# Summing the squares of a norm on TensorE instead of VectorE, in a two-layer diffusion block on one core

## The chip, the core and the metric

The kernel runs on one NeuronCore of a Trainium2 chip. A core has five engines that work in parallel, each through its own queue in order: PE (TensorE, the matrix engine; the loads of its stationary operand are shown apart as PEld), DVE (VectorE), ACT (ScalarE), POOL (GpSimd) and SP (SyncE, which issues the transfers here). They wait for each other by semaphores. PE writes into PSUM, which has eight banks of 128 x 512 floats; the other data lie in SBUF, 128 partitions wide. The metric is the device time of one execution in microseconds (us), the median over several.

## The reference, cut to what matters

The program is one pass of a small diffusion backbone: 512 latent and 256 context tokens of width 1024, two layers. Layer 0 mixes tokens by gated linear attention, layer 1 by neighbourhood attention; each is followed by a gated MLP with a width-3 convolution. Ahead of each of the four sub-layers, and at the end, stands an RMS norm:

```
def rms_norm(x, g):
    xf = x.astype(jnp.float32)
    y = xf * lax.rsqrt(jnp.mean(xf * xf, axis=-1, keepdims=True) + EPS)
    return (y * g.astype(jnp.float32)).astype(x.dtype)

def modulate(x, g, shift, scale):
    return rms_norm(x, g) * (1 + scale) + shift
```

In layer 1 the context tokens are only read, so that from there on the norms cover the 512 latent tokens alone. All is computed in float32.

## The kernel before, in words

Activations lie transposed: features on the partitions, tokens along the free axis. The 1024 features are eight tiles of 128 rows, so a norm has to sum eight squares elementwise and then sum over the 128 partitions. Weight products are made in three passes of a split operand (high and low parts, `mm3`, lines 274 to 277): each product that the text names is three matmuls, L275, L276 and L277.

The class `Norm` does the norms, for a range of tokens of width w = 512 or 256. There are ten of them at five places: before the linear attention (latent 512, then context 256), before the first MLP (`finish_gla`), between the first MLP and the neighbourhood stage (`last_outs(0, ...)`), between the neighbourhood stage and the second MLP (two halves of 256 latent tokens), and the final norm (two halves of 256).

`add(k)` is called when tile k of x is final: ACT squares it (L320 straight into the sum `nacc` for the first tile, L323 into a scratch tile `sq` for the other seven), and DVE adds each of those seven into the sum (L324). At two of the places the sum is a part of a tile named `apad`, and the scratch tiles are T2h, T3h, T4l and the like. `stats()` sums over the partitions on PE: for each 128 tokens one matmul with the squares as stationary operand and two columns of ones as moving operand (L331; each such float32 matmul is two records in the trace). Then DVE scales (`ms`, L333), POOL takes the power -0.5 (`rs`, L335), PE spreads the result over the partitions by a product with the identity (L338), and at the start ACT copies it to SBUF (`rb`, L342). `apply(k)` multiplies and splits tile k into the `hh` and `hl` of the next products (DVE L358, ACT L359, DVE L360).

At the places within the program the tile of x is made by a product on PE, added to the residual by DVE (`add_gated`, L299), squared by ACT, and so on; the norm of one range is applied while the products of the next range run (`todo`). L147, L150, L155 and L128 belong to `ada_first`, which makes the first layer's shift and scale; L270 and L271 split weight tiles into their high (`wh`, ACT) and low (`wl`, DVE) parts; L234 and L145 are transfers of weights.

The order on each engine is not that of the source: the framework that builds the program schedules it by its own estimate of durations, and each engine then runs its list strictly in order. So an edit in the norm also moves instructions around it. Scratch tiles and PSUM banks rotate; the norm at the start has four scratch tiles.

## Time and profile before

| what | value |
|---|---|
| time, median of 3 runs | 1723.74 us |
| the three runs | 1716.87, 1723.74, 1723.84 us |
| profiled execution, its own time | 1716.47 us |
| span of its trace | 1714.7 us |
| PE busy | 96% of the span |
| DVE, ACT, POOL busy | 69%, 43%, 12% |

In the rows below, a timeline row reads: start in us, duration in us (of a merged row, from the first start to the last end), engine, line, operation, out<-in, shape, count, and in brackets how long the engine sat idle before it and which instruction ended that. A window row gives busy time and count for PE, PEld, DVE, ACT and POOL, then the granted TensorE clock, the share of busy transfer engines and GB/s. Matmuls are pipelined: a product on 256 columns is shown as 0.28 us long, but the next one starts 0.12 us later.

### The profile page before, as it was taken

Reading aid. Unit: us, or ns where it says so; the run is one execution under the profiler, and the core shown is the slowest. Engines: PE = TensorE matmul, PEld = TensorE weight load, DVE = VectorE, ACT = ScalarE, POOL = GpSimd, SP = SyncE. Lnnn points to the kernel's source line nnn. Section 1 sums busy time; section 2 is a strip of 40 time slices with the busy share of each in tenths; the row PEclk is TensorE's granted clock in tenths of the full one; section 3 lists DMA queues with packets and bytes.
Section 4 is the critical chain, followed back from the end, with each engine's and each line's share of the span. In section 5 each row is a group of like instructions: output and inputs, shape, how many; then the busy total and the mean of one; then the engine's idle time right before and its main releaser. Section 6 shows DMA issues by size and latency. Waiting matters only on the chain.

```text
span 1714.7 us, 27141 instructions
## 1 busy us (share of the span) xinstructions
PE 1648.3 (96%) x10867; PEld 1412.8 (82%) x10867; DVE 1187.9 (69%) x1973; ACT 740.0 (43%) x1331; POOL 206.6 (12%) x321
## 2 busy tenths in 40 slices
PE   5999999999999999999999989999999999999997
PEld 3768778777899999999999868887877888888887
DVE  4797877775997877978767774647476755555555
ACT  3665756563753342433434543433344522222332
POOL 1031212320000000000000042433332000000000
PEclk9999999999999999999999989999999999999999
DMA  7653523014333332524223051415141232322321
GB/s 259 193 173 101 172 73 107 20 50 136 99 120 113 114 109 74 172 64 145 89 72 110 26 192 48 147 47 160 43 135 38 85 96 91 99 87 86 110 86 50
DMA packets 54190, 179.70 MB, mean 105 GB/s; under 512 B 7024, under 2 KB 10864, under 8 KB 54064
## 3 DMA queue, kind: packets, MB, share of 16 engines
q1 hardware_dynamic: 54064, 177.97, 32.5%
q8 instruction: 85, 1.39, 0.3%
q14 instruction: 41, 0.34, 0.1%
HBM read 173.75 MB, written 2.10 MB: 103 GB/s over the span
## 4 chain that ended last, share of the span: by engine, by line
PE 72%; DVE 11%; ACT 5%; issue 4%; DMA 4%; POOL 3%; SPq 0%; POOLq 0%; DVEq 0%; ACTq 0%
PE mm L275 14%; PE mm L276 14%; PE mm L277 14%; PE aux L275 8%; PE aux L276 8%; PE aux L277 8%; DMA sa<-in 2%; PE mm L1236 1%; PE aux L1219 1%; POOL bias L1132 1%; PE aux L637 1%; DVE acc L200 1%; DVE t L558 1%; PE aux L1194 1%; DMA st<-in 1%
## 5 line engine op out<-in xcount | busy, mean ns | idle before, releaser
L275 PE MATMUL mm<-hh,wl 128*128 128x512 f32 (+3 forms) x864 | 307.2, 358 | 4.6 <-ACT hh L359 2.5
L276 PE MATMUL mm<-hl,wh 128*128 128x512 f32 (+3 forms) x864 | 302.2, 350 | 0.0
L277 PE MATMUL mm<-hh,wh 128*128 128x512 f32 (+3 forms) x864 | 301.9, 350 | 0.0
L275 PE MATMUL mm<-uh,wl 128*128 128x512 f32 (+1 forms) x544 | 189.0, 349 | 0.0
L276 PE MATMUL mm<-ul,wh 128*128 128x512 f32 (+1 forms) x544 | 188.8, 347 | 0.2 <-DVE ul L288 0.2
L277 PE MATMUL mm<-uh,wh 128*128 128x512 f32 (+1 forms) x544 | 188.9, 348 | 0.0
L275 PEld LDWEIGHTS mm<-hh,wl 128*128 128x128 f32 (+1 forms) x864 | 163.1, 189 | 28.9 <-issue 5.0
L270 ACT ACTIVATE wh<-st 128x1024 fp32r<-128x1024 f32 (+1 forms) x127 | 131.8, 1051 | 114.8 <-issue 69.4
L299 DVE SCALAR_TENSOR_TENSOR xl<-mm,mod,xl 128x512 f32<-128x512 f32 (+1 forms) x168 | 116.2, 698 | 93.8 <-PE mm L277 92.9
L276 PEld LDWEIGHTS mm<-hl,wh 128*128 128x128 f32 (+1 forms) x864 | 163.7, 189 | 18.0 <-issue 1.0
L277 PEld LDWEIGHTS mm<-hh,wh 128*128 128x128 f32 (+1 forms) x864 | 163.3, 189 | 18.1 <-issue 0.4
L275 PE MATMUL aux<-hh,wl 128*128 128x384 f32 (+2 forms) x496 | 173.7, 351 | 0.0
L276 PE MATMUL aux<-hl,wh 128*128 128x384 f32 (+2 forms) x496 | 173.6, 350 | 0.0
L277 PE MATMUL aux<-hh,wh 128*128 128x384 f32 (+2 forms) x496 | 173.4, 350 | 0.0
L271 DVE TENSOR_TENSOR wl<-st,wh 128x1024 fp32r<-128x1024 f32 (+1 forms) x126 | 153.8, 1227 | 22.7 <-ACT wh L270 22.3
L250 ACT ACTIVATE wh<-st 128x512 fp32r<-128x512 f32 (+1 forms) x126 | 94.1, 756 | 164.9 <-issue 56.9
L335 POOL TENSOR_TENSOR rs<-ms,mhalf 128x2 f32<-128x2 f32 (+1 forms) x10 | 10.9, 1094 | 930.8 <-DVE ms L333 930.8
L275 PEld LDWEIGHTS mm<-uh,wl 128*128 128x128 f32 x544 | 102.8, 189 | 15.7 <-ACT uh L287 2.0
L276 PEld LDWEIGHTS mm<-ul,wh 128*128 128x128 f32 x544 | 103.0, 189 | 14.7 <-DVE ul L288 0.4
L277 PEld LDWEIGHTS mm<-uh,wh 128*128 128x128 f32 x544 | 102.8, 189 | 13.2
L251 DVE TENSOR_TENSOR wl<-st,wh 128x512 fp32r<-128x512 f32 (+1 forms) x126 | 104.7, 848 | 13.0 <-ACT wh L250 12.7
L275 PEld LDWEIGHTS aux<-hh,wl 128*128 128x128 f32 x496 | 93.5, 189 | 8.6 <-issue 1.2
(330 smaller groups left out, 3251.3 us busy)
## 6 DMA issues: line engine op xcount, KB each, us to landing
st<-in SPq DMA_DIRECT2D x201, 512.0 KB, 3.7
sa<-in SPq DMA_DIRECT2D x98, 512.0 KB, 4.1
sx<-in SPq DMA_DIRECT2D x14, 512.0 KB, 6.3
xl<-in SPq DMA_DIRECT2D x8, 512.0 KB, 6.5
xc<-in SPq DMA_DIRECT2D x4, 512.0 KB, 8.4
out<-y SPq DMA_DIRECT2D x16, 128.0 KB, 1.7
raw<-in SPq DMA_DIRECT2D x16, 96.0 KB, 2.5
t<-q SPq DMA_DIRECT2D x16, 64.0 KB, 2.2
```

The source lines that it names most:

```text
L200: nc.vector.scalar_tensor_tensor(acc[0], st, cs[:, k, c:c + 1], acc[0], OP.mult, OP.add)
L250: nc.scalar.activation(hi, s_, AF.Copy)
L251: nc.vector.tensor_sub(lo, s_, hi.bitcast(F32))
L270: nc.scalar.activation(hi, st, AF.Copy)
L271: (eng or nc.vector).tensor_sub(lo, st, hi.bitcast(F32))
L275: mm(out, a[1], b[0], start=first, stop=False, **at)
L276: mm(out, a[0], b[1], start=False, stop=False, **at)
L277: mm(out, a[0], b[0], start=False, stop=last, **at)
L299: nc.vector.scalar_tensor_tensor(x_, ps, gate(l, n, d, rng), x_, OP.mult, OP.add)
L558: nc.vector.tensor_mul(ek, ek, st[h]["k"])
L637: mm(ps[:, 0:DV], a_, b_, start=i == 0, stop=i == len(terms) - 1)
L1132: nc.gpsimd.tensor_tensor(bt[ps_, o2:o2 + 192], rv[ps_], nmask[ps_, var, 64 * half:64 * half + 192], OP.add)
```

## The change

The sum of the squares may now be made in PSUM. A new method `total` issues the matmuls with ones; PE accumulates over several of them in one bank. In most norms six squares are still added on DVE and the eighth is handed to PE by itself, so that `stats` issues two groups of matmuls, one on the sum and one on the last square. At the place between the neighbourhood stage and the second MLP (`pe=True`) there is no DVE sum at all: each of the eight squares gets its own group as soon as it is there. The tile `nacc` is not allocated there.

```diff
         def add(self, k):
 
-            if self.first:
-                self.first = False
+            self.count += 1
+            if self.count == 1 and not self.pe:
                 if self.acc is None:
                     self.acc = self.pool.tile([128, self.w], F32, name="nacc", tag=f"nacc{self.w}", bufs=2)
                 nc.scalar.activation(self.acc, xk(k, self.rng), AF.Square)
                 return
             sq = self.tmp("sq")
             nc.scalar.activation(sq, xk(k, self.rng), AF.Square)
-            nc.vector.tensor_add(self.acc, self.acc, sq)
+            if self.pe:
+                self.total(sq)
+            elif self.count < KD:
+                nc.vector.tensor_add(self.acc, self.acc, sq)
+            else:
+                self.last = sq
+
+        def total(self, sq, last=False):
+
+            first = self.ps is None
+            if first:
+                self.ps = ps_aux()
+            for i in range(self.w // 128):
+                mm(self.ps[:, 2 * i:2 * i + 2], sq[:, i * 128:(i + 1) * 128], ones, start=first and i == 0,
+                   stop=last or self.count == KD and self.pe, skip_group_check=True)
 
         def stats(self):
 
             c = self.w // 128
-            ps = ps_aux()
-            for i in range(c):
-                mm(ps[:, 2 * i:2 * i + 2], self.acc[:, i * 128:(i + 1) * 128], ones, start=True, stop=True)
+            if not self.pe:
+                self.total(self.acc)
+                self.total(self.last, True)
+            ps = self.ps
...
         todo = []
-        nacc = pool.tile([128, D], F32, name="nacc", tag="acc", bufs=1)
         for a, b in ((0, 256), (256, 512)):
-            norm = Norm(pool, 1, 1, (N_CTX + a, N_CTX + b), acc=nacc[:, a:b])
+            norm = Norm(pool, 1, 1, (N_CTX + a, N_CTX + b), pe=True)
             for d in range(KD):
                 out_group(3, d, a, b)
```

In the changed file the lines of `Norm` lie lower: L331 becomes L339, L338 becomes L355, L323 becomes L325, L342 becomes L359 and L359 becomes L376.

How the order moves, first on PE at the start of the program, before (`nacc` is the sum, `rs` the reciprocal root, `sx` the weights of the first shift and scale):

```order
L331 MATMUL aux<-ones,nacc 128x2 x4
L338 MATMUL aux<-ident,rs_160 128x128 x4
L331 MATMUL aux<-ones,nacc 128x2 x2
L147 MATMUL mm<-sx,cs 32x256
L338 MATMUL aux<-ident,rs_197 128x128 x2
L147 MATMUL mm<-sx,cs 32x256 x15
```

and now:

```order
L339 MATMUL aux<-ones,nacc 128x2 x4
L339 MATMUL aux<-ones,sq 128x2 x4
L355 MATMUL aux<-ident,rs_163 128x128 x4
L339 MATMUL aux<-ones,nacc 128x2 x2
L339 MATMUL aux<-ones,sq 128x2 x2
L147 MATMUL mm<-sx,cs 32x256
L355 MATMUL aux<-ident,rs_201 128x128 x2
L147 MATMUL mm<-sx,cs 32x256 x15
```

Each group on the sum is followed by an equal group on the last square, and all else stands as it did.

On ACT at the same place, before (xc_81 and xc_82 are the context tiles, `rb` the copy of the spread root):

```order
L320 ACTIVATE nacc<-xc_81 128x256
L323 ACTIVATE sq<-xc_81 128x256 x3
L323 ACTIVATE sq<-xc_82 128x256 x4
L342 ACTIVATE rb<-aux 128x512
L270 ACTIVATE wh<-st 128x512
L342 ACTIVATE rb<-aux 128x256
```

and now:

```order
L322 ACTIVATE nacc<-xc_81 128x256
L325 ACTIVATE sq<-xc_81 128x256 x3
L325 ACTIVATE sq<-xc_82 128x256 x2
L359 ACTIVATE rb<-aux 128x512
L325 ACTIVATE sq<-xc_82 128x256 x2
L270 ACTIVATE wh<-st 128x512
L359 ACTIVATE rb<-aux 128x256
```

The last two squares of the context range now stand behind the copy of the latent range's root.

On ACT between the neighbourhood stage and the second MLP, in the second half of the tokens, now (`xl` are the latent tiles, two features' tiles in each; the squares of the second half begin in the first row; before, single squares and single `hh` rows took turns here):

```order
L325 ACTIVATE sq<-xl_4196 128x256 x2
L376 ACTIVATE hh<-hf,mod_120 128x256 x2
L325 ACTIVATE sq<-xl_4197 128x256 x2
L376 ACTIVATE hh<-hf,mod_120 128x256
L325 ACTIVATE sq<-xl_4198 128x256
L376 ACTIVATE hh<-hf,mod_120 128x256
L270 ACTIVATE wh<-st 128x1024
L325 ACTIVATE sq<-xl_4198 128x256
L270 ACTIVATE wh<-st 128x1024
L376 ACTIVATE hh<-hf,mod_120 128x256 x2
L325 ACTIVATE sq<-xl_4199 128x256 x2
L376 ACTIVATE hh<-hf,mod_120 128x256 x10
```

Two weight copies (`wh`) now stand between the fourth and the fifth `hh`, with one square between them.

## The prediction

> **What bounds the kernel now.** I read the engines' share of the span first, then the chain of work that ended last, then the instructions at each of the five places with a norm.

> ```profile
> span 1714.7 us, 27141 instructions
> PE 1648.3 (96%) x10867; PEld 1412.8 (82%) x10867; DVE 1187.9 (69%) x1973; ACT 740.0 (43%) x1331; POOL 206.6 (12%) x321
> PE 72%; DVE 11%; ACT 5%; issue 4%; DMA 4%; POOL 3%; SPq 0%; POOLq 0%; DVEq 0%; ACTq 0%
> ```

> PE is busy 96% of the span and carries 72% of the chain; DVE, which the change relieves, is busy 69% and carries 11%. So work that moves from DVE to PE costs time wherever PE does not wait, and can only pay where PE waits for DVE. Such places are the start, the stretch between the neighbourhood stage and the second MLP, and the last microseconds. At the start the chain of waits, read in order of time, passes through the norm itself:

> ```profile
> 12.58 0.70 DVE nacc L324
> ...
> 13.41 1.85 PE aux L331 x8
> ...
> 18.53 0.44 DVE nacc L324
> 19.01 1.03 PE aux L331 x4
> ...
> 21.45 1.22 PE aux L338 x4
> 22.67 3.60 PE mm L147 x30
> ...
> 28.50 0.76 DVE hf L358
> ```

> The reader is to see that no slack lies here: the last latent add, its matmuls with ones (eight records), the last context add and its four records, the spread root (L338), and only then the products for the first shift (L147), since PE takes them in order; the first `hf` of the program (28.50) hangs on these.

> **The start.** Timeline rows of the same stretch, and its window:

> ```profile
> 15.37 3.59 DVE L324 TENSOR_TENSOR nacc<-nacc,sq 128x256 f32<-128x256 f32 x7
> 15.53 1.12 POOL L335 TENSOR_TENSOR rs<-ms,mhalf 128x4 f32<-128x4 f32 x1 [14.44 <-DVE ms L333]
> 16.70 2.07 PE L338 MATMUL aux<-ident,rs 128*128 128x128 f32 x8 [1.46 <-POOL rs L335]
> 18.81 0.60 ACT L342 ACTIVATE rb<-aux 128x512 f32<-128x512 f32 x1 [1.52 <-PE aux L338]
> 13.00:21.00 8.00, 5.90 (x22) 4.67 (x22) 4.09 (x11) 2.83 (x7) 1.81 (x2) 1.00 1.02 408
> ```

> Latent range: one add of 0.70 goes, and a second group of eight records comes, as long as the first (1.85). So its end, 15.26, moves by -0.70 + 1.85 = +1.15. The scale and the power (1.12) and the eight records of L338 (2.07) follow it, and the copy `rb` ends at 18.81 + 0.60 + 1.15 = 20.56 instead of 19.41. Context range: its seven adds ended at 18.96 and did not care about `rb`, because ACT made all seven squares before that copy. In the new order the last two squares stand behind it on ACT. So square six ends at about 20.56 + 0.42 = 20.98, the sixth add (0.44) at 21.4, and two groups of four records (1.03 each) end at 23.5, where one ended at 20.04. That is **+3.4** on the path to L147 and so to everything behind it. If ACT had kept its order, the context adds would start 1.15 later, be one fewer, and the extra group would give 1.15 - 0.44 + 1.03 = +1.7.

> This rests on 0.23 per record (1.85 by 8). Later in the program a group of four takes 0.36, 0.09 per record (1327.09 to 1327.45 in the next fence). With 0.09 the latent end moves by -0.70 - 1.85 + 16 x 0.09 = -1.1, `rb` ends at 18.3, square six at 18.7, its add at 19.2, eight records at 19.9: -0.1. These are the ends, -0.1 and +3.4; I take +3.4, because the slow rows are at this very place. The clock column of the window speaks for the other end: it shows 1.00 granted. [...]

> **Between the neighbourhood stage and the second MLP.** Timeline rows of PE and ACT, and two windows:

> ```profile
> 1323.00 0.39 PE L275 MATMUL mm<-oh,wl 128*128 128x256 f32 x1 [0.31 <-DVE xl L299]
> ...
> 1327.09 0.50 PE L331 MATMUL aux<-ones,nacc 128*128 128x2 f32 x4
> 1327.45 0.37 PE L275 MATMUL mm<-oh,wl 128*128 128x256 f32 x1
> 1327.65 0.28 PE L276 MATMUL mm<-ol,wh 128*128 128x256 f32 x1
> 1327.77 0.28 PE L277 MATMUL mm<-oh,wh 128*128 128x256 f32 x1
> ...
> 1328.64 0.71 PE L338 MATMUL aux<-ident,rs 128*128 128x128 f32 x4 [0.35 <-POOL rs L335]
> ...
> 1332.90 0.39 PE L275 MATMUL mm<-oh,wl 128*128 128x256 f32 x1 [1.66 <-DVE xl L299]
> ...
> 1333.56 1.06 ACT L270 ACTIVATE wh<-st 128x1024 fp32r<-128x1024 f32 x1 [0.20 <-PE mm L277]
> ...
> 1334.51 0.35 PE L275 MATMUL mm<-hh,wl 128*128 128x256 f32 x1 [0.63 <-DVE xl L299]
> 1334.53 0.49 ACT L359 ACTIVATE hh<-hf,mod 128x256 fp32r<-128x256 f32 x1
> ...
> 1341.42 0.71 PE L338 MATMUL aux<-ident,rs 128*128 128x128 f32 x4 [1.25 <-POOL rs L335]
> ...
> 1327.00:1342.00 15.00, 11.10 (x87) 10.24 (x86) 12.85 (x33) 8.22 (x18) 2.32 (x2) 1.00 0.03 3
> 1342.00:1356.00 14.00, 14.00 (x119) 14.00 (x118) 10.89 (x22) 6.87 (x14) 0.19 (x4) 1.00 0.26 78
> ```

> The price of one group on 256 tokens: it starts at 1327.09, the next product at 1327.45, and the one behind that 0.20 later instead of the usual 0.12 (1327.65 to 1327.77). So a group takes 0.36 to 0.44 of PE, and I use 0.40. There were two groups, there are sixteen: 14 x 0.40 = 5.6. Each of the 14 adds that go takes 0.43 on DVE (row in the last fence), but that pays only where PE waited for DVE: 0.31, 1.66 and 0.63, together 2.6. The brackets count from the modelled end of the product before (0.28 after its start) although the next could have started after 0.12, so each wait is 0.16 longer in truth: 3.1. With DVE free of the adds and PE slower I expect all three to go. The two waits for the power (0.35 and 1.25) stay, as POOL is as fast as before; the second shrinks by 0.24, because six products stand between its groups and L338 now, four before.

> One wait is new. The weight copies of ACT wait for a slot that one of the last products of this stage frees (1333.56). Before, `hh` and squares stood between the two copies; now, between the fourth and the fifth `hh`, come a copy, one square, a copy: 1.06 + 0.42 + 1.06, then 0.49 for the `hh`, 3.0 in all after the slot comes free. Behind it on ACT are the sixth `hh` and the last two squares, and DVE's `hl` waits for each `hh`. PE needs that fifth `hh` after some 16 products and a group, 16 x 0.12 + 0.40 = 2.3. So PE waits 0.7 for `hh`, and about as long again as that `hh` (0.5) for the `hl` that follows; part of that is absorbed if PE is late by then. I take 1.0. Sum: 5.6 - 3.1 - 0.2 + 1.0 = **+3.3**. Ends: 14 x 0.36 = 5.0, less all waits for DVE and POOL (3.1 + 1.6) = +0.3; 14 x 0.44 = 6.2 with the new wait at 1.4 and no wait removed = +7.6. Nothing behind absorbs it: in the window from 1342 to 1356 PE is busy 14.00 of 14.00.

> **Ahead of the first MLP, and behind it.** Rows of PE at these norms:

> ```profile
> 425.59 0.95 PE L331 MATMUL aux<-ones,apad 128*128 128x2 f32 x8
> 426.39 0.36 PE L275 MATMUL mm<-hh,wl 128*128 128x256 f32 x1
> 426.60 0.28 PE L276 MATMUL mm<-hl,wh 128*128 128x256 f32 x1
> ...
> 452.93 0.58 PE L331 MATMUL aux<-ones,apad 128*128 128x2 f32 x4 [0.70 <-DVE apad L324]
> 454.78 0.71 PE L338 MATMUL aux<-ident,rs 128*128 128x128 f32 x4 [0.26 <-POOL rs L335]
> ...
> 964.06 1.46 PE L338 MATMUL aux<-ident,rs 128*128 128x128 f32 x8 [0.82 <-POOL rs L335]
> ...
> 983.34 0.71 PE L338 MATMUL aux<-ident,rs 128*128 128x128 f32 x4 [1.20 <-POOL rs L335]
> ...
> 964.00:966.00 2.00, 1.94 (x12) 1.94 (x13) 0.82 (x2) 0.00 (x0) 0.01 (x1) 0.69 0.00 0
> 966.00:968.00 2.00, 2.00 (x11) 2.00 (x11) 1.36 (x4) 1.72 (x3) 0.00 (x0) 0.50 0.00 0
> ```

> Ahead: the latent group (eight records) takes 425.59 to 426.60 less 0.12 = 0.89, and PE does not wait there for the sum, so +0.9. The context group waited 0.70 for its sum and 0.26 for the power, 1.3 with the correction of about 0.16 each. Now the group on the sum stands some 15 products earlier, five products lie between it and the square, and 15 more ahead of L338: both waits go, and 0.40 comes: -0.9. Together 0.0. Behind: latent +0.89, less 0.24 because six products instead of four cover the power (0.82 idle); context +0.40, less 0.7 because six products on 512 columns (twice 0.12 each) instead of three cover it (1.20 idle): **+0.4** together. Between -1 and +2.

> **The end.** The last rows of the chain:

> ```profile
> 1704.38 0.42 ACT L323 ACTIVATE sq<-xl 128x256 f32<-128x256 f32 x1 [1.00 <-DVE xl L299]
> 1704.83 0.43 DVE L324 TENSOR_TENSOR nacc<-nacc,sq 128x256 f32<-128x256 f32 x1
> 1705.31 0.61 PE L331 MATMUL aux<-ones,nacc 128*128 128x2 f32 x4 [1.54 <-DVE nacc L324]
> ```

> The last add leaves the path: the group on the square can start at 1704.85 instead of 1705.31, and that on the sum has run before. -0.45; the first half of the final norm gets a group among PE's products, +0.1. **-0.35**, between -0.6 and 0.

> **Sum.** 3.4 + 0.0 + 0.4 + 3.3 - 0.35 = +6.8. The profiled execution took 1716.47 (span 1714.7 and 1.8 around it), so it would take 1723.3. But the runs shown lie on two levels, 1716.9 and 1723.8, and the profile on the lower one. With the mean of these four, 1720.2, I predict **1727.0**, 0.4% more than before, inside the 0.5% (8.6 us) that a measurement of this kernel can tell from no change.

> **The rivals.**

> - *ACT's queue decides the stretch ahead of the second MLP* (slower). The copies and squares ahead of the fifth `hh` hold PE, and waits for DVE only change their name. Price +7.6 there, 3.4 + 0.4 + 7.6 - 0.35 = +11.1, 1731.3. For it: ACT is in order, and the slot comes free only with the last product. Against: ACT is busy only 8.22 of the 15.00 from 1327 to 1342. It decides from the point at which PE reaches the fifth `hh` sooner than 3.0 after the slot is free. 0.25.
> - *The start runs at full pace.* -0.1 there instead of +3.4: +3.3, 1723.5. For it the clock column, against it the rows. 0.12.
> - *DVE was the bound.* All waits in that stretch go, and the start is at its low end: -0.1 + 0.4 + 0.3 - 0.35 = +0.3, 1720.5. 0.08.
> - *A clock dip goes away.* The window 964 to 966 shows 0.69 granted, the next one 0.50, right behind a wait of 0.82. At half clock for some 4 us PE loses about 2.0. A shorter wait may spare it: +4.8, 1725.0. 0.10. [...]

> The forecast has 0.40; 0.05 is left for a reordering that I have not priced (the lists differ for some stretches into the first MLP too).

> **How the numbers follow.** The low end, 1718, holds the low-end case and the lower level of the runs; the high end, 1736, the ACT rival with the upper level of the runs (1723.8 + 11.1 = 1734.9). Slower by over 0.5%: most of the first rival and the forecast's upper tail, 0.30. Faster by over 0.5% needs a gain that no row offers, or a change of level: 0.06. The rest, 0.64, is within 0.5%.

> **What would show it.** Right: two equal groups of ones back to back at 12 to 16 us; the first `hf` at about 31.9 instead of 28.5; PE busier between 1317 and 1345 with no wait for `xl`, yet the second MLP starting some 7 us later than before; a new wait of a product for `hh` or `hl` there; the last scale (L333) 0.5 sooner after its last square. Wrong: a start under 1 us later than before, records of 0.09 at the start, or waits for `xl` that stay. The prediction falls if the whole is under 1718, that is if PE's added groups are hidden behind waits that I have put down to DVE.

## The result and the profile after

The changed kernel takes 1730.64 us (median of 9 runs, 1725.08 to 1731.48), the kernel before 1721.98 us (median of 9, 1716.87 to 1725.65). The ratio is 1.0044, with a 95% interval of 1.003 to 1.0057, or +5.2 to +9.8 us. Predicted were 1727.0 us and +6.8 us over the runs then known. The profiled execution of the changed kernel took 1730.82 us.

The top of its page and the shares of the chain that ended last:

```profile
span 1729.0 us, 27308 instructions
PE 1661.9 (96%) x10967; PEld 1428.0 (83%) x10967; DVE 1180.0 (68%) x1951; ACT 740.4 (43%) x1331; POOL 206.3 (12%) x321
PE 72%; DVE 11%; ACT 5%; issue 4%; DMA 3%; POOL 3%; SPq 0%; POOLq 0%; DVEq 0%; ACTq 0%
```

DVE has 22 instructions and 7.9 us of work fewer, PE 100 records and 13.6 us more. The shares of the chain are what they were, but for DMA (3% for 4%): nothing was won by the relief of DVE.

At the start, timeline rows of the changed kernel that answer to the chain shown in the prediction:

```profile
12.52 1.84 PE L339 MATMUL aux<-ones,nacc 128*128 128x2 f32 x8 [7.77 <-DVE nacc L329]
14.22 1.84 PE L339 MATMUL aux<-ones,sq 128*128 128x2 f32 x8
17.52 2.08 PE L355 MATMUL aux<-ident,rs 128*128 128x128 f32 x8 [1.45 <-POOL rs L352]
19.63 0.60 ACT L359 ACTIVATE rb<-aux 128x512 f32<-128x512 f32 x1 [2.58 <-PE aux L355]
20.12 0.71 ACT L325 ACTIVATE sq<-xc 128x256 f32<-128x256 f32 x2
21.04 1.01 PE L339 MATMUL aux<-ones,nacc 128*128 128x2 f32 x4 [1.45 <-DVE nacc L329]
21.92 0.99 PE L339 MATMUL aux<-ones,sq 128*128 128x2 f32 x4
25.49 3.64 PE L147 MATMUL mm<-sx,cs 128*32 128x256 f32 x30
31.39 0.75 DVE L375 SCALAR_TENSOR_TENSOR hf<-xl,modA,rb 128x512 f32<-128x512 f32 x1
```

The two equal groups back to back, the last two context squares behind `rb`, and the two context groups that wait for them are all there, and the first `hf` comes at 31.39 instead of 28.50.

Between the neighbourhood stage and the second MLP, the waits of PE, and the window from the first product on 256 columns to the first product on `uh` of the second MLP, first in the kernel before:

```profile
PE mm L275 <- DVE xl L299: 2.6, 3, 1.7
PE aux L338 <- POOL rs L335: 1.6, 2, 1.3
PE mm L275 <- ACT oh L287: 0.7, 1, 0.7
1317.22:1371.11 53.89, 49.03 (x354) 45.79 (x352) 44.44 (x91) 28.73 (x54) 2.51 (x6) 1.00 0.28 83
```

and in the changed one (a row of waits gives the total, how often, and the longest):

```profile
PE aux L355 <- POOL rs L352: 1.5, 2, 1.1
PE mm L275 <- ACT oh L287: 0.7, 1, 0.7
1329.14:1385.46 56.32, 54.20 (x409) 51.62 (x408) 40.73 (x77) 28.65 (x54) 2.50 (x6) 1.00 0.27 80
```

All three waits for `xl` have gone, and no wait for `hh` or `hl` has come. PE has 5.17 us more of work in this stretch and 2.74 us less of waiting, so the stretch is 2.43 longer.

Ahead of the first MLP, rows of PE, DVE and POOL in the changed kernel, and the window of one stretch at half clock there:

```profile
435.85 2.07 PE L355 MATMUL aux<-ident,rs 128*128 128x128 f32 x8 [0.86 <-POOL rs L352]
...
461.25 0.75 DVE L377 SCALAR_TENSOR_TENSOR hl<-R,mod,hh 128x512 fp32r<-128x512 f32 x1
461.91 0.16 DVE L350 TENSOR_SCALAR ms<-aux 128x2 f32<-128x2 f32 x1
462.15 1.88 POOL L352 TENSOR_TENSOR rs<-ms,mhalf 128x2 f32<-128x2 f32 x1 [3.99 <-DVE ms L350]
464.08 0.71 PE L355 MATMUL aux<-ident,rs 128*128 128x128 f32 x4 [0.70 <-POOL rs L352]
...
435.89:439.31 3.42, 3.42 (x16) 3.42 (x17) 1.35 (x3) 0.56 (x1) 0.00 (x0) 0.50 0.71 259
```

PE no longer waits for the sum, as predicted, but the wait for the power has grown from 0.26 to 0.70: the scale `ms` stands behind an `hl` on DVE, and the power took 1.88. And PE is at half clock for 3.42 us.

At the end:

```profile
1718.64 0.61 PE L339 MATMUL aux<-ones,nacc 128*128 128x2 f32 x4
1719.15 0.42 ACT L325 ACTIVATE sq<-xl 128x256 f32<-128x256 f32 x1 [1.02 <-DVE xl L299]
1719.62 0.61 PE L339 MATMUL aux<-ones,sq 128*128 128x2 f32 x4 [0.37 <-ACT sq L325]
```

The last group starts 0.05 after its square ends, where before 0.51 lay between (1704.80 to 1705.31). That is the -0.45 of the prediction.

**Where the time went, over all traces.** One pair of traces misleads here. In the first pair the changed kernel lost 4.9 us between its first product of q and k (70.86 before, 72.60 after) and its first group of ones ahead of the first MLP (425.59 and 432.22), where the order of no engine differs. So I cut every trace of this study at the same nine marks; the table has nine of the fourteen traces. The columns are the time from one mark to the next: the first `hf`; the first product of `wh` and `hl` (q and k); the first group of ones ahead of the first MLP; its first product on `uh`; the first product on `PT` in the neighbourhood stage; the first output product on 256 columns; the first product on `uh` of the second MLP; the last record of ones; the end. The kernels are those of the experiments below.

| trace | hf | q, k | ones | uh | PT | 256 | uh, 2nd | last ones | end |
|---|---|---|---|---|---|---|---|---|---|
| before | 28.50 | 42.36 | 354.73 | 83.87 | 512.74 | 295.02 | 53.89 | 334.56 | 9.02 |
| before, again | 27.30 | 42.03 | 354.57 | 85.41 | 512.39 | 295.24 | 55.29 | 334.70 | 9.66 |
| start alone changed | 31.39 | 42.54 | 355.84 | 83.56 | 512.62 | 299.88 | 55.30 | 334.75 | 9.02 |
| changed | 31.39 | 41.21 | 359.62 | 86.32 | 514.14 | 296.47 | 56.32 | 334.51 | 9.04 |
| changed, again | 30.33 | 42.20 | 356.97 | 86.30 | 513.21 | 298.42 | 56.32 | 334.51 | 9.04 |
| changed, norms around the first MLP as before | 30.52 | 42.21 | 355.22 | 83.92 | 512.36 | 296.63 | 56.32 | 334.38 | 9.03 |
| changed, stretch ahead of the second MLP as before | 30.66 | 42.22 | 355.22 | 84.75 | 513.40 | 299.73 | 53.88 | 334.25 | 10.53 |
| changed, start as before | 28.32 | 42.48 | 355.72 | 83.84 | 513.23 | 297.38 | 56.26 | 334.35 | 9.57 |
| changed, old order at the start | 28.64 | 42.09 | 354.85 | 84.77 | 515.04 | 296.50 | 56.28 | 334.40 | 9.02 |

Some of the cells with equal code differ by 1.4 to 5 us. In many of these the granted clock is 0.50 for one or two stretches of about 3.4 us more, which is part of the difference and not all of it: the stage from `PT` to 256 took 295.02 with such a stretch at 1186.6 us and 295.24 without one. Such stretches lie at 292.5, 364.2 and 435.9 us in the first trace of the changed kernel, at 362.0 and 433.7 in its second, at 426.9 and 1334.9 in the second trace of the kernel before, and at none of these places in its first.

### The profile page after: what moved, and what is told of

Same layout as the page of the kernel before. It is cut to its first block, busy times and chain, and to the rows that moved or that the text cites. A ratio compares the mean times of both kernels' runs of the same rounds, so it can differ in the third digit from the quotient of the medians.

```text
span 1729.0 us, 27308 instructions
## 1 busy us (share of the span) xinstructions
PE 1661.9 (96%) x10967; PEld 1428.0 (83%) x10967; DVE 1180.0 (68%) x1951; ACT 740.4 (43%) x1331; POOL 206.3 (12%) x321
## 4 chain that ended last, share of the span: by engine, by line
PE 72%; DVE 11%; ACT 5%; issue 4%; DMA 3%; POOL 3%; SPq 0%; POOLq 0%; DVEq 0%; ACTq 0%
PE mm L275 14%; PE mm L276 14%; PE mm L277 14%; PE aux L275 7%; PE aux L277 7%; PE aux L276 7%; DMA sa<-in 2%; PE mm L1253 1%; PE aux L1236 1%; POOL bias L1149 1%; DVE acc L200 1%; PE aux L654 1%; DVE t L575 1%; PE aux L1211 1%; DVE wl L271 1%
## 5 line engine op out<-in xcount | busy, mean ns | idle before, releaser
L275 PE MATMUL mm<-hh,wl 128*128 128x512 f32 (+3 forms) x864 | 308.0, 358 | 4.0 <-ACT hh L376 2.5
L277 PE MATMUL mm<-hh,wh 128*128 128x512 f32 (+3 forms) x864 | 302.8, 351 | 0.0
L276 PE MATMUL mm<-hl,wh 128*128 128x512 f32 (+3 forms) x864 | 302.8, 351 | 0.0
L275 PE MATMUL mm<-uh,wl 128*128 128x512 f32 (+1 forms) x544 | 189.3, 349 | 0.8 <-ACT uh L287 0.7
L276 PE MATMUL mm<-ul,wh 128*128 128x512 f32 (+1 forms) x544 | 188.9, 348 | 0.0
L277 PE MATMUL mm<-uh,wh 128*128 128x512 f32 (+1 forms) x544 | 188.6, 348 | 0.0
L275 PEld LDWEIGHTS mm<-hh,wl 128*128 128x128 f32 (+1 forms) x864 | 163.7, 190 | 27.6 <-issue 3.7
L299 DVE SCALAR_TENSOR_TENSOR xl<-mm,mod,xl 128x512 f32<-128x512 f32 (+1 forms) x168 | 116.3, 698 | 97.2 <-PE mm L277 96.6
L270 ACT ACTIVATE wh<-st 128x1024 fp32r<-128x1024 f32 (+1 forms) x127 | 131.8, 1050 | 115.4 <-issue 69.6
L276 PEld LDWEIGHTS mm<-hl,wh 128*128 128x128 f32 (+1 forms) x864 | 164.2, 190 | 17.9 <-issue 1.0
L277 PEld LDWEIGHTS mm<-hh,wh 128*128 128x128 f32 (+1 forms) x864 | 164.0, 190 | 18.0 <-issue 0.4
L275 PE MATMUL aux<-hh,wl 128*128 128x384 f32 (+2 forms) x496 | 173.9, 351 | 0.0
L276 PE MATMUL aux<-hl,wh 128*128 128x384 f32 (+2 forms) x496 | 173.5, 350 | 0.0
L277 PE MATMUL aux<-hh,wh 128*128 128x384 f32 (+2 forms) x496 | 173.4, 350 | 0.0
L271 DVE TENSOR_TENSOR wl<-st,wh 128x1024 fp32r<-128x1024 f32 (+1 forms) x126 | 153.6, 1225 | 21.9 <-ACT wh L270 21.4
L275 PEld LDWEIGHTS mm<-uh,wl 128*128 128x128 f32 x544 | 102.4, 189 | 17.3 <-ACT uh L287 2.9
L276 PEld LDWEIGHTS mm<-ul,wh 128*128 128x128 f32 x544 | 102.5, 188 | 14.6 <-DVE ul L288 0.2
L277 PEld LDWEIGHTS mm<-uh,wh 128*128 128x128 f32 x544 | 102.4, 188 | 13.2
L275 PEld LDWEIGHTS aux<-hh,wl 128*128 128x128 f32 x496 | 93.6, 189 | 8.5 <-issue 1.2
```

Source lines behind the costliest of these rows:

```text
L270: nc.scalar.activation(hi, st, AF.Copy)
L271: (eng or nc.vector).tensor_sub(lo, st, hi.bitcast(F32))
L275: mm(out, a[1], b[0], start=first, stop=False, **at)
L276: mm(out, a[0], b[1], start=False, stop=False, **at)
L277: mm(out, a[0], b[0], start=False, stop=last, **at)
L299: nc.vector.scalar_tensor_tensor(x_, ps, gate(l, n, d, rng), x_, OP.mult, OP.add)
```

## The experiments

Each ratio is to the kernel before, timed beside it on the same chip. In the expectations, the stretch ahead of the second MLP is counted to a product on `uh` some 6.6 us behind the first one, which the table uses; so 59.5 and 62.0 there are 53.9 and 56.3 here.

### The start as before

```diff
-        norms = [Norm(pool, 0, 0, rng, spread=True) for rng in (LAT, CTX)]
+        norms = [Norm(pool, 0, 0, rng, spread=True, old=True) for rng in (LAT, CTX)]
...
-            elif self.count < KD:
+            elif self.old or self.count < KD:
...
-                self.total(self.acc)
-                self.total(self.last, True)
+                self.total(self.acc, self.old)
+                if not self.old:
+                    self.total(self.last, True)
```

> The changed kernel with the two norms at the start summed as before (seven adds on VectorE, one group of ones); the other eight norms as changed. My step (start +3.4, measured +2.89 at the first hf: 28.50 before, 31.39 after): the first hf comes back to 28.5, and the whole is 1.7 to 3 us below the changed kernel, that is 4 to 7 us over the kernel before (the changed one was 8.7 over it by medians). 1.7 and not 2.9 if the clock decides: in both traces TensorE came back to full clock at the same time (36.34 before, 36.53 after), and at 40 us only 1.75 of the 2.89 was left. Rival (the start is hidden behind the weights that arrive later): total as the changed kernel, 8 to 9 over before. A second question: on all engines the order up to the first MLP is now the same as before. If the 4.9 us that the changed kernel lost between 40 and 420 us (at 121, 158, 288 and 358 us, in lists that the change does not touch) came from the later start, they vanish here; if they are a matter of the single execution, some of them may be here too, at places of their own.

Measured: ratio 1.0002 (0.9987 to 1.0017), that is -2.2 to +2.9 us. The first `hf` is back at 28.32 and the first q and k product at 70.80 (70.86 before). By the ratios that is some 7 us below the changed kernel, more than twice what was foreseen; the run of the start alone, below, says why this can't be read as the price of the start. From q and k to the ones the trace shows 355.72: of the 4.9 us, 1.0 is still there, without a half-clock stretch.

In this trace the wait for the power ahead of the first MLP does not occur, though the order of all engines at that place is that of the changed kernel. POOL's row:

```profile
454.88 0.95 POOL L353 TENSOR_TENSOR rs<-ms,mhalf 128x2 f32<-128x2 f32 x1 [3.98 <-DVE ms L351]
```

The same power took 0.95 here and 1.88 above. Of the ten traces with the new sums at this place, eight have 1.88 or 1.89 and two 0.95; the four with the old sums have 0.94 or 0.95.

### The stretch ahead of the second MLP as before

```diff
-            norm = Norm(pool, 1, 1, (N_CTX + a, N_CTX + b), pe=True)
+            norm = Norm(pool, 1, 1, (N_CTX + a, N_CTX + b), acc=nacc[:, a:b], old=True)
```

> The changed kernel with the two norms between the neighbourhood stage and the second MLP summed as before on VectorE (a sum on VectorE, one group of ones per half); all else, and the order of every engine up to there, as changed. My step (+3.3 for this stretch; measured +2.47 from the first product on 256 columns to the products on uh of the second MLP, 59.5 before and 62.0 after): the stretch goes back to 59.5, three waits of TensorE for xl (0.31, 1.66, 0.63) are back, and the whole is 2 to 3.5 us below the changed kernel, some 5 to 6.5 over before. Rival (ACT's queue decides there: the waits for xl only change their name): the stretch stays at 62. Rival (VectorE was the bound, the removed waits pay for the groups): the stretch and the total do not move, or get longer.

Measured: ratio 1.003 (1.0016 to 1.0044), +2.8 to +7.6 us. The stretch is 53.88 long, 0.01 from the kernel before. My step holds in the trace: this part costs 2.4 us, and the second MLP behind it is not longer for it (334.25 to the last ones here, 334.51 in the changed kernel; only the last stores took 1.5 longer in this one trace). Both rivals fall by the length of the stretch. The total lies where it was foreseen, but its interval overlaps that of the changed kernel, so that it does not show the 2.4 by itself.

### The old order at the start, with the new sums

```diff
         for norm in norms:
             for k in range(KD):
                 norm.add(k)
+        for norm in norms:
             norm.stats()
```

> The changed kernel with one thing moved: at the start all sixteen squares are asked for ahead of the two sums over the partitions. By this the last two context squares stand ahead of the copy rb on ScalarE again, as before the change; the added groups of ones stay. (The first two shift products also stand behind the spread of the second root.) My step: with ScalarE's old order the start is +1.7 instead of +3.4: the first hf at about 30.0 to 30.3 (28.50 before, 31.39 after), and the total 0 to 1.5 us below the changed kernel. Rival (the groups of ones are the whole delay, order plays no part): the first hf stays at 31.4. Rival (TensorE's slow records do not matter, order is all): first hf at 28.5.

Measured: ratio 1.0027 (1.0013 to 1.0041). Timeline rows:

```profile
10.00 1.15 ACT L325 ACTIVATE sq<-xl 128x512 f32<-128x512 f32 x2 [0.19 <-DMA xl<-in]
...
15.73 1.96 ACT L325 ACTIVATE sq<-xc 128x256 f32<-128x256 f32 x4 [3.18 <-PE aux L339]
...
19.21 0.60 ACT L359 ACTIVATE rb<-aux 128x512 f32<-128x512 f32 x1 [1.52 <-PE aux L355]
...
22.17 1.22 PE L355 MATMUL aux<-ident,rs 128*128 128x128 f32 x4 [1.42 <-POOL rs L352]
...
23.32 3.04 PE L147 MATMUL mm<-sx,cs 128*32 128x256 f32 x32
...
28.64 0.75 DVE L375 SCALAR_TENSOR_TENSOR hf<-xl,modA,rb 128x512 f32<-128x512 f32 x1
```

The four squares stand ahead of `rb`, and the first `hf` is at 28.64, 0.14 from the kernel before, with all the added groups in place. But the input came earlier in this trace. The same two latent squares in the kernel before, and in the changed one:

```profile
10.48 1.15 ACT L323 ACTIVATE sq<-xl 128x512 f32<-128x512 f32 x2 [0.20 <-DMA xl<-in]
10.44 1.15 ACT L325 ACTIVATE sq<-xl 128x512 f32<-128x512 f32 x2 [0.20 <-DMA xl<-in]
```

From the end of these squares to the first `hf` are 17.49 us here, 16.87 in the kernel before (16.09 and 16.81 in the two other traces of the table with the old start) and 19.80 in the changed kernel. So ACT's order makes 2.3 of the delay and the groups alone 0.6 to 1.4, and my +1.7 for them was too high. The groups put the spread of the second root at 22.17 instead of 21.45, +0.72; but the shift products behind it run as one block of 32 in 3.04 and end at 26.36, where before 30 of them took 3.60 and ended at 26.27. How long these products take hangs on when the clock rises: 30 took 2.89 in the second trace of the kernel before, where it rose at 24.1 us and not at 26.1. The time of the whole, on the other hand, is not clearly below that of the changed kernel.

### A busy TensorE ahead of the first norm

```diff
+    warm = ps_aux()
+    for i in range(20):
+        mm(warm[:, 128 * (i % 4):128 * (i % 4) + 128], ident, ident, start=True, stop=True)
+
     cs = cst.tile([128, KD, 32], F32, name="cs")
```

> The changed kernel with 20 products of the identity by itself (128 columns each, into a PSUM bank that nobody reads) put on TensorE ahead of the first norm, where it waits for x from 4.6 to 12.5 us; else nothing moves on any engine. [...] Rival (the slow records are a property of the shape or of reading the squares, the clock is full as the profile's column says): records of 0.21 stay, the 20 products take 0.43 each and end at 13.2, and the first hf is late by a further 0.7. Rival (the clock falls again in the waits of 1 to 1.5 us between the groups): the first groups are fast, the later ones slow, and less than 2 us is gained.

Measured: ratio 1.0023 (1.0009 to 1.0036). Timeline rows, and the windows of the first 26 records of that filling (L105 has run before), of the first and of the later groups of ones:

```profile
12.23 1.02 PE L342 MATMUL aux<-ones,nacc 128*128 128x2 f32 x8 [0.75 <-DVE nacc L332]
13.12 1.03 PE L342 MATMUL aux<-ones,sq 128*128 128x2 f32 x8
17.04 0.60 ACT L362 ACTIVATE rb<-aux 128x512 f32<-128x512 f32 x1 [4.35 <-PE aux L358]
17.53 1.32 ACT L328 ACTIVATE sq<-xc 128x256 f32<-128x256 f32 x4
19.51 1.01 PE L342 MATMUL aux<-ones,nacc 128*128 128x2 f32 x4 [2.51 <-DVE nacc L332]
...
4.40:9.55 5.15, 5.15 (x26) 5.15 (x26) 3.10 (x7) 3.20 (x7) 0.00 (x0) 1.00 1.02 398
12.23:14.10 1.87, 1.86 (x16) 1.83 (x16) 0.00 (x0) 0.46 (x2) 0.00 (x0) 1.00 1.02 407
19.50:21.20 1.70, 1.69 (x8) 1.69 (x8) 0.00 (x0) 0.00 (x0) 0.00 (x0) 0.50 0.79 313
```

The eight records of the first group take 1.02 instead of 1.84, so it is the clock, and not their shape, that makes the records at the start long. But the clock fell again at 16.4, and the later groups took 1.01 for four records at 0.50 granted. So the rival in which the clock falls again holds: the first `hf` comes at 29.45, 1.5 us before the mean of the traces with the changed start (30.9). Against what was expected, an order moved too: on ACT four context squares stand behind `rb` here (the row at 17.53), where the changed kernel has two. The last context add ends 2.42 us after the start of `rb` and not 1.36, so that some 1.1 us can be lost there beside the slow groups; this run does not separate the two. The total is some 3.6 us below the changed kernel by the ratios, but the intervals overlap. And the clock column can't be read at the start of a trace: it says 1.00 for 4.40 to 9.55, where a record takes 0.20 (26 in 5.15), and for 12.23 to 14.10, where it takes 0.12 (16 in 1.87).

### Both kernels once more

No edit: the two kernels as they are, for second traces.

> The kernel before, unchanged, for a second trace of it. Theory (the 4.9 us that the changed kernel's trace lost between 40 and 420 us, and the 3.0 at 1270 to 1290, are chance of single executions: transfers that land a little later, and half-clock stretches of 3.4 us that fall at other places): the stretches with equal lists differ from the first trace by 0.5 to 4 us here too, the half-clock stretches beside those at 30, 965 and 1020 us lie elsewhere, and the time is anywhere from 1715 to 1726. Rival (they are an effect of the change): the second trace agrees with the first within 0.5 us in each of these stretches.

> The changed kernel, unchanged, for a second trace of it. Theory (chance, as in the run beside it): first hf near 31 (31.39 in the first trace), 62.9 us again between the neighbourhood stage and the second MLP, but of the 4.9 us lost between 40 and 420 us most is not there (the kernel with the same lists up to 1318 us and the old sum behind it lost 0.7 in that stretch). Rival (the change causes it): 4 to 5 us are lost there again, with half-clock stretches near 292 and 364 us.

Measured: 1718.38 and 1729.11 us. The second trace of the kernel before differs from the first by 1.5 us ahead of the first MLP and by 1.4 ahead of the second, with stretches of half clock at 426.9 and 1334.9. The window of the stretch ahead of the second MLP in that trace:

```profile
1316.93:1372.22 55.29, 50.32 (x354) 47.16 (x352) 44.52 (x91) 28.73 (x54) 2.51 (x6) 0.97 0.28 81
```

0.97 granted and 55.29 us, where the first trace has 1.00 and 53.89: in this trace a half-clock stretch lies among the waits for `xl`. From q and k to the ones, however, the two traces of the kernel before agree within 0.2, as the rival has it, and the second trace of the changed kernel lost 2.2 us there, not 4.9 and not 0.7, with one half-clock stretch (362.0) instead of two. So neither expectation is met in full.

### The norms around the first MLP as before

```diff
-        lat, cx = Norm(pool, 0, 1, LAT, acc=acc[:, N_CTX:T], **at), Norm(pool, 0, 1, CTX, acc=acc[:, 0:N_CTX], **at)
+        lat, cx = Norm(pool, 0, 1, LAT, acc=acc[:, N_CTX:T], old=True, **at), Norm(pool, 0, 1, CTX, acc=acc[:, 0:N_CTX], old=True, **at)
...
-                              lambda rng: Norm(pool, 1, 0, rng, blocks=rng == LAT, acc=apad[:, rng[0]:rng[1]],
+                              lambda rng: Norm(pool, 1, 0, rng, old=True, blocks=rng == LAT, acc=apad[:, rng[0]:rng[1]],
```

> The changed kernel with the four norms around the first MLP (ahead of it, and behind it ahead of the neighbourhood stage) summed as before; the start, the stretch ahead of the second MLP and the end as changed. My step (0.0 ahead of the first MLP, +0.4 behind it): total as the changed kernel within 1 us. By the traces so far (ahead of it +0.9 where the clock did not fall, since the second wait for the power grew from 0.26 to 0.70; behind it -0.7 to +0.5): 0 to 1.5 us below the changed kernel; the stretch from 422 to 457 us is 34.3 long instead of 35.2. Rival (these places carry the rest of the 8.7): 3 us or more below.

Measured: ratio 1.003 (1.0016 to 1.0043), +2.8 to +7.4 us. From the ones to `uh` the trace has 83.92, from there to `PT` 512.36, as with the old sums elsewhere. The new sums cost some 0.7 and 1.0 there, beside half-clock stretches. By the ratios the total is 2.4 us below the changed kernel, between the 0 to 1.5 foreseen and the rival's 3, and the intervals overlap: this run does not rule out that these places carry more than their traces show.

### The shift ahead of the second norm

```diff
         for norm in norms:
             for k in range(KD):
                 norm.add(k)
-            norm.stats()
+        norms[0].stats()
+        shift = ada_first(0, pool)
+        norms[1].stats()
...
-        ada_first(0, pool)()
+        shift()
```

with the old sums at the start and ahead of the second MLP.

> A version meant to beat both: at the start and ahead of the second MLP the old sums (the two places where the added groups cost), at the other places the new ones, and the products for the first shift and scale (32 records on TensorE, whose weights have all landed by 18.8 us) are asked for ahead of the second norm's sum over the partitions, so that they fill TensorE's waits between 16 and 22 us instead of standing behind the whole norm at 22.6 to 26. Theory (the first hf hangs on the shift, which waits for nothing but its place in TensorE's queue): first hf at about 26 instead of 28.5, total 1 to 3 us below the kernel before. Rival (what is gained there is lost again, since the clock comes back to full only at about 36 us, or since the later shift weights set the pace): at 40 us less than 0.5 is left, total within 1 us of the kernel before.

Measured: ratio 0.9998 (0.9989 to 1.0008). The first `hf` came at 30.11, not at 26: half of the 32 records did move ahead, but PE did not come to full clock before 38.0 in that trace (26.1 in the first of the kernel before), the last record ended at 26.5 (26.3 before), and what follows ran at half clock. The rival, no gain, holds.

### The start alone changed

The kernel before with the changed start; all other norms `old=True`.

> The kernel before with the change at the start alone (a second group of ones for each of the two norms, six adds instead of seven); the other eight norms on VectorE as before. By this the two last context squares stand behind rb on ScalarE, as in the changed kernel; no other order moves. Theory from the traces (start +2.9 at the first hf, +2.3 at 40 us, and 0.6 more at a wait for xl at 158 us that all traces with a late start show): 2 to 3.5 us over the kernel before, first hf at 30.3 to 31.4. Rival from the times (the changed kernel is 7 to 8.7 over before, and with the old start only 0.3 over): the start carries 6 to 8 us, of which most arises behind 40 us. Rival (undoing it gained by chance): below 2 us.

Measured: ratio 1.0012 (0.9999 to 1.0024), -0.2 to +4.1 us, and the first `hf` at 31.39. This speaks for the theory from the traces, 2 to 3.5, and against 6 to 8; the third case, below 2, lies within the interval. The start alone at +2.1 and all but the start at +0.3 do not add up to the +7.6 of the whole (all by ratios): 5.2 us are missing, and the three intervals together, taken as independent, leave some 4.

### The groups ahead of the second MLP twice

```diff
+            if self.pe:
+                for i in range(self.w // 128):
+                    mm(self.ps[:, 256 + 2 * i:258 + 2 * i], sq[:, i * 128:(i + 1) * 128], ones, start=False,
+                       stop=self.count == KD, skip_group_check=True)
```

> The changed kernel with each of the sixteen groups of ones between the neighbourhood stage and the second MLP issued twice, the second time into columns that nobody reads; the order of all else is the same. It measures the price of a group there by itself. Theory (a group takes 0.36 to 0.44 of TensorE, and nothing hides it since TensorE is the bound there): the stretch from the first product on 256 columns to the products on uh becomes 62.9 + 16 x 0.40 = 69.3 us long (68.7 to 70.0), less what falls into the two waits for the power (1.5 in all, behind the last groups, so nothing). Rival (part of it falls into waits): 66 or less.

Measured: 1754.25 us in one run, and 84.14 us for the stretch instead of 62.7 (69.3 by the mark of the expectation). What PE waited for there, the window of the stretch, and the 3.41 us ahead of the fall of the clock:

```profile
PE mm L275 <- ACT oh L287: 0.7, 1, 0.7
PE aux L359 <- POOL rs L356: 0.5, 1, 0.5
1324.93:1409.07 84.14, 83.04 (x473) 80.29 (x472) 41.19 (x77) 28.78 (x54) 2.51 (x6) 0.72 0.18 53
1328.97:1332.38 3.41, 3.41 (x32) 3.41 (x32) 1.44 (x2) 0.69 (x2) 0.00 (x0) 1.00 0.57 213
```

PE is busy 83.04 of 84.14 us, and yet 0.72 is granted: the clock stood at half from 1332.4 to 1380.2. In the 3.41 us ahead of the fall PE had no gap at all. By the start times of its rows (1328.96 to 1329.40, 1329.84 to 1330.65, 1331.21 to 1332.02), 2.05 of the 3.41 us went to groups of ones. Neither theory foresaw this.

### Wide products in the place of the second groups

```diff
+            if self.pe:
+                for i in range(self.w // 128):
+                    mm(self.ps[:, 256:384], ident, ident, start=False,
+                       stop=self.count == KD and i == 1, skip_group_check=True)
```

> The changed kernel with two products of the identity by itself (128 columns each, four records, into columns that nobody reads) behind each of the sixteen groups of ones between the neighbourhood stage and the second MLP, in place of the doubled group of the run between_double; they take about as long (0.11 per record, 0.44 for four). Some products and copies change places around them. Question: with the doubled groups TensorE had no gap from 1326 to 1378 us and yet was granted half clock for 47.8 us (1332.4 to 1380.2), so that the stretch took 90.7 us in place of 69. Theory (the grant follows how many columns stream through the array and not whether TensorE has an instruction: a group of ones streams 2 columns per load, and with two thirds of the time on such groups the clock falls): with products of 128 columns in the same time the clock stays at 1.00 and the stretch is 62.9 + 16 x 0.44 = 70 us (68 to 72), the total about 1737. Rival (the clock fell by chance, or for any added work there, the whole chip's power for one): half clock for some 40 us again, stretch 85 or more.

Measured: 1738.85 us in one run. The window of the stretch:

```profile
1328.52:1393.16 64.64, 62.22 (x473) 59.04 (x472) 40.83 (x77) 28.77 (x54) 2.51 (x6) 1.00 0.23 69
```

As many records as with the doubled groups (473), but 1.00 granted and 64.64 us. The theory holds in this pair: where the added records move two columns the stretch was granted 0.72, with PE busy for 83.04 of 84.14 us, and where they move 128 it was granted 1.00. Each of the two runs is a single execution; the last section counts the same thing over all traces.

### A busy TensorE through the whole start

The shift ahead of the second norm, as above, and fillers:

```diff
+    def fill(n):
+        t = ps_aux()
+        for i in range(n):
+            mm(t[:, 128 * (i % 4):128 * (i % 4) + 128], ident, ident, start=True, stop=True)
+
+    fill(24)
...
+            if self.spread:
+                fill(6 if self.w == 512 else 4)
             pb = ps_aux()
...
+        shift()
+        fill(12)
```

> A version meant to beat both kernels: the old sums at the start and ahead of the second MLP, the new ones at the other places; the products for the first shift and scale asked for ahead of the second norm's sum; and products of the identity by itself, which nobody reads, in TensorE's waits at the start (24 ahead of the first norm, 6 and 4 in the two waits for the power, 12 ahead of the first product on hh). Theory (the start is long because TensorE runs at half clock to 26 us and again from 30 to 36, which these traces show by records of 0.21 instead of 0.11, and because the shift products stand behind the norm): groups of eight ones records in 0.9 us instead of 1.84, first hf at 24 to 26 instead of 28.5, no half clock from 30 to 36, 3 to 6 us below the kernel before at 40 us and in the total. Rival (in order, the fillers stand in the way as often as they help, or the clock falls all the same): within 1.5 us of the kernel before. [...]

Measured: median 1717.07 us, ratio 0.9969 (0.9958 to 0.9979), -7.2 to -3.6 us. It beats both kernels. Rows of its start, and the window from the first product on `hh` to 38 us:

```profile
13.27 1.23 PE L346 MATMUL aux<-ones,nacc 128*128 128x2 f32 x8 [2.02 <-DVE nacc L336]
14.35 2.91 PE L112 MATMUL aux<-ident 128*128 128x128 f32 x12
25.63 0.74 DVE L385 SCALAR_TENSOR_TENSOR hf<-xl,modA,rb 128x512 f32<-128x512 f32 x1
...
27.58:38.00 10.42, 10.32 (x73) 6.45 (x74) 6.14 (x10) 2.67 (x4) 2.65 (x1) 1.00 0.54 172
```

The same window of the kernel before has 0.67 granted and 36 records of PE, this one 1.00 and 73. The first group of ones took 1.23 and not 0.9, since the clock fell to half once more from 13.9 to 17.3. The first `hf` comes at 25.63, and the first q and k product at 65.27 instead of 70.86: the gain of 5.6 arises at the start, and the total is 5.3 lower by the ratio. The run of the shift ahead of the second norm, which is this one without the fillers, had no gain (0.9998): the fillers make it.

## Why the prediction was right, point by point

The total, +6.8, lies inside the measured +5.2 to +9.8, and the ratio of 1.0044 is just inside the 0.5% on which most of the chance, 0.64, stood; its interval reaches to 0.57%. An interval of 1.003 to 1.0057 also tells the change from none, which the prediction had held to be too small for that; and the two levels on which it had put the runs are not there, since nine runs of the kernel before are spread over 1716.87 to 1725.65. The terms of the sum were less good than the sum, and that the sum came out is partly luck: the start and the stretch ahead of the second MLP were put 0.8 and 1.8 too high, and 0.6 and 1.2 more than foreseen came around the first MLP and 2.0 at a place that had no term. The last column here is the difference of the means over the traces with the old and with the new code at each place, from the table and the traces of the other runs:

| place | predicted | first pair | over the traces |
|---|---|---|---|
| start, to the first q and k product | +3.4 | +1.7 | +2.6 |
| q and k to the first MLP, equal orders | 0 | +4.9 | +2.0 |
| ahead of the first MLP, to its `uh` | 0.0 | +2.4 | +1.2 |
| behind it, to `PT` | +0.4 | +1.4 | +1.0 |
| ahead of the second MLP | +3.3 | +2.4 | +1.5 |
| end, to the last ones | -0.35 | -0.05 | -0.3 |

(The start is the mean of seven traces with the changed start, 72.9, less that of the two of the kernel before and the one with the old start, 70.3. The second row is the same seven, 357.0, against seven without it, 355.0. In the others six to ten traces stand on the side of the new sums and three to six on that of the old. The neighbourhood stage, with equal orders, took 295.0 to 300.2 on both sides and is left out; it is 1.5 of the 14.3 in the first pair.) They add to +8.0.

- **The start.** The mechanism is the one that was priced: slow records (1.84 us for eight of ones, 1.02 with a busy TensorE ahead of them) and two squares behind `rb`. At the first `hf` it is +2.9 in the mean (30.9 against 28.0). What failed is the side step "if ACT had kept its order, +1.7": with the old order it is +0.14 at the first `hf`, and +0.6 to +1.4 counted from the end of the latent squares. I had carried the delay of the groups on to the first `hf` one for one, and had not asked at which clock the 32 products behind them would run. That the records there can be fast shows in the runs with a busy TensorE: records fell from 0.21 to 0.11 us after 5.8 us of unbroken work in the first of them (3.73 to 9.55) and after 3.4 in the other (3.78 to 7.17). In the changed kernel they were not, 1.84 for each eight: the rival of a full pace falls.
- **Ahead of the first MLP.** The failed step is "both waits go". The wait for the sum went, 0.70; that for the power grew to 0.70, with `ms` behind `hl` on DVE and a power of 1.88. It is the length of the power that makes it: where it took 0.95 in the same order, PE waited 0 (start as before) or 0.28 (busy TensorE). Both lengths occur with the same three DVE instructions beside the power. The runs show the two lengths and not their cause. Without a half-clock stretch this place costs 0.7, of which the latent +0.9 was priced.
- **Behind it.** +0.4 was mis-sized, +1.0 with a spread of 3 us between traces, wider than the term.
- **Ahead of the second MLP.** 5.6 for the groups and -3.1 for the waits for `xl` were right: 2.43 in the trace, plus 3.1 and the 0.1 that came off the waits for the power, is 5.6, or 0.40 a group. The failed term is the new wait for `hh`, +1.0: the first four `hh` serve the products of two weight blocks, so that more work lay ahead of the fifth than the 16 products I had counted, and no wait for `hh` or `hl` came. A second thing was missed: of six traces with the old sums four have a half-clock stretch here, which costs 1.4 us, and of six with the new sums none (the last section has the work of PE in the thinnest 3.41 us there). So the change removes more than the waits, and costs 1.5 rather than 2.4 in the mean.
- **The end.** -0.3, as priced.
- **The rivals.** ACT's queue did not decide, since no product waited for `hh`; the time itself, 1730.64, is nearer to that rival's 1731.3 than to 1727.0. DVE was not the bound: its waits went, and the groups cost more than they gave. The dip at 964 went in some traces of the changed kernel and stayed at 966.6 or 964.9 in others with the same or part of the change; half-clock stretches did not go away, they moved, and there are six ahead of the end in both traces of the changed kernel, where the kernel before has four.

**What stays open.** From q and k to the first MLP, where no order differs, seven traces with the late start take 355.2 to 359.6, and seven without it 354.6 to 355.7. Four of the seven late ones have one or two half-clock stretches there (near 292 and 362 to 364 us), none of the others has. The place near 360 is as thin in both kernels (0.91 us of wide work in its thinnest 3.41 us before, 0.87 after, counted as in the last section); why it fell only with the late start is not shown, and the seven are too few to rule out chance. And the times of the parts do not add to the whole: the start alone +2.1, all but the start +0.3, the whole +7.6 by ratios, more than their intervals allow if they are independent. The runs of the experiments come from three chips; whether that matters is not shown either.

## What to carry to other kernels

A matmul with a column or two of moving data is a dear way to use TensorE: a group costs 0.40 us for two 128 x 128 squares here, and with sixteen groups more TensorE was granted half clock for 47.8 us, though it had no gap in the 3.41 us ahead of the fall. Before work is moved to a busy engine, ask which of its waits will go and which will only be handed on: here the waits for VectorE went, but were worth less than the instructions that came. And where a span begins with microseconds of half clock, cheap wide products in the first waits can be worth more than the tuning of the chain behind them: -5.3 us here, against +7.6 for the change, both by ratios.
